# Tile places modulo 256 bytes, fifteen products of ones at the start, and the first weights ahead of the second part of x, in a two-layer encoder kernel

## The chip, the cores and the metric

The kernel runs on one core of a Trainium2 chip, in one launch. A core has TensorE (PE, matrix products; its weight loads are listed apart as PEld), VectorE (DVE), ScalarE (ACT), GpSimd (POOL) and SyncE (SP, which here issues all DMAs). The engines run side by side and wait for each other through semaphores. The metric is the device time of one execution in microseconds (us); lower is better.

## The reference, cut to what matters

Two layers on x of 512 tokens by 1024 features, all fp32. A layer has three attention branches, gates that mix them, and a squared-ReLU FFN:

```python
for l in range(2):
    h = rms_norm(x, norm_mix[l])
    u = h @ w_in[l]                               # one product, split into all that follows
    qa, ka, va, fa, qd, kvd, kr, qc, kc, vc, gl = split(u)
    ya = forgetting_attention(rms(qa), rms(ka), va, cumsum(log_sigmoid(fa + b)))
    yb = latent_attention(rms(qd) @ w_q_up, rms(kvd) @ w_kv_up, rope(kr))
    yc = chunk_attention(rms(qc), rms(kc), vc, rel_bias)
    merged = sum(sigmoid(gl_n + b_gate_n) * (y_n @ w_branch[n]))   # n = A, B, C
    x = x + merged @ w_out[l]
    h = rms_norm(x, norm_ffn[l])
    x = x + square(relu(h @ w_ff1[l])) @ w_ff2[l]
```

## The kernel before, in words

Each fp32 operand is split into a rounded high part and the rest (hi and lo, xgh and xgl, ah and al, mh and ml, yh and yl), both of type fp32r. A product of two split operands is three PE products of 128x128 weights with 512 moving columns: hi by hi, hi by lo, lo by hi. About 7000 of them make up the kernel.

All weight matrices lie in one DRAM array in the order of their use. `take` (line 127) brings the next 512 KB piece into a tile raw (line 137), ACT writes its rounded copy to whi (line 140) and DVE the rest to wlo (line 141). PE's program order is the order of the code; the other engines' order comes from a scheduler that goes by priorities. Tiles come from pools in SBUF (128 partitions; a tile takes the same bytes in each): the constants, w (raw, whi, wlo), xg (xgh, xgl: x times the norm's gain), t2 (temporaries), sm (small ones), and behind them pools that come and go with the stages: y and mg, mix, m (mh, ml), act (ah, al). A pool starts where the one before it ends, so the size of an earlier one sets where a later one lies. Two pools on the right side (xi, x) are placed from the other end.

The stages of a layer: projections for branch A (PE names ps_t, ps_k), the row norms (token sums ps_sum, line 292; then ps_r, line 320, which spreads them over the partitions with the constant onesr as weights and the tiles dg moving); attention A, C and B, each with gate tiles (ps_f), score products (ps_s), transposes (ps_p, ps_q), value products (ps_y) and branch projections (ps_b, line 802) between; the merge, which is the branch projection of B and the output projection (ps_o); and the FFN. In the FFN, 16 tiles of the first product (ps, moving xgh and xgl) alternate with 8 tiles of the second (ps, moving ah and al), twice a layer.

In most products the weights are the streamed tile (whi, wlo) and the activations move; in ps_t it is the other way round, xgh and xgl are the weights and whi, wlo move.

The program's start is in `run` (line 1000): SP issues the gains (vec), then the eight parts of x (xi, 256 KB each), with three prefetched weight pieces between (line 1018); the first piece comes in two halves. ACT and DVE split each part of x (`norm_split`, lines 272 and 273) and each weight piece. The first 72 products need three pieces and six parts of x, with the first piece used one part of x at a time.

Of the kernel before, what the change touches and what calls it, by code (L numbers as in the profile page):

```python
# [9 lines left out]
F32 = mybir.dt.float32  # L10
# [8 lines left out]
P = 128  # L19
T = 512  # L20
# [29 lines left out]
V_MIX, V_FFN, V_BG = 0, 8, 16  # L50
# [10 lines left out]
TUNE = dict(  # L61

    mla='ddddddddddddubuubu0qqqbbqqqqqbbuuuubqbbb1kbbktkkkbbbkkkbtbbgg',

    over=[1.0, 1.0, 1.0],

    na=10,

    tv=[13, 24],

    st=[0, 2, 4],

# [30 lines left out]
class Stream:  # L103


    def __init__(self, k, ap, layer):
        self.k, self.ap, self.layer, self.at, self.keys, self.pre = k, ap, layer, 0, [], []
# [39 lines left out]
class Fill:  # L147
# [10 lines left out]
    def run(self, ns):  # L158
        self.owed += ns
        while self.q and self.owed > 0:  # L160
            try:
                self.owed -= next(self.q[0])
            except StopIteration:
                self.q.pop(0)
        if not self.q:
            self.owed = 0.0
# [10 lines left out]
class Kern:  # L177
    def __init__(self, tc, ctx, a):
        self.tc, self.nc, self.a = tc, tc.nc, a
        self.ahead = TUNE["ahead"]  # L180
        self.fine = False
        self.ctx = ctx
        self.pc = self.pool(ctx, "const", 1)
        self.pw = self.pool(ctx, "w", 3)
        self.px = self.pool(ctx, "xg", 8)
        self.t2 = self.pool(ctx, "t2", 6)
        self.sm = self.pool(ctx, "sm", 2)
        self.dr = self.pool(ctx, "dr", 1, space=DRAM)
        self.mm = self.pool(ctx, "mm", 3, space=PSUM)
        self.pS = self.pool(ctx, "ps", 2, space=PSUM)  # L190
        self.pt = self.pool(ctx, "pt", 2, space=PSUM)
        self.py = self.pool(ctx, "py", 1, space=PSUM)

        self.sm.tile([P, 56], F32, tag="pad", name="pad", bufs=1)
        self.streams = [Stream(self, a["w"], l) for l in range(DEPTH)]
        self.vec = self.pc.tile([P, DEPTH, NV], F32, name="vec")

# [15 lines left out]
    def consts(self):  # L213
        nc, pc = self.nc, self.pc
        c = self.tmp()
        nc.sync.dma_start(out=c, in_=self.a["cst"])
        self.ident = pc.tile([P, P], F32, name="ident")
        self.li = pc.tile([P, 32], F32, name="li")
        nc.vector.memset(self.li, 0.0)
        nc.vector.tensor_copy(out=self.ident, in_=c[:, 0:128])  # L220
        self.maska = pc.tile([P, P], F32, name="maska")
        nc.vector.tensor_copy(out=self.maska, in_=c[:, 128:256])
        self.onesr = pc.tile([P, P], F32R, name="onesr")
        nc.vector.tensor_copy(out=self.onesr, in_=self.ones)
        self.hb = pc.tile([P, DEPTH, 24], F32, name="hb")
        nc.vector.tensor_scalar(out=self.hb, in0=self.vec[:, :, V_BG : V_BG + 24], scalar1=0.5, scalar2=None, op0=ALU.mult)
# [773 lines left out]
    def run(self):  # L1000
        nc = self.nc
        self.xd = self.dr.tile([P, KT, T], F32, name="xd")
        self.norm_begin()
        with ExitStack() as ctx:
            p0 = self.pool(ctx, "x0", 1, side="right")
            xs = [p0.tile([P, T], F32, name=f"xi{kt}") for kt in range(KT)]
            ahead, self.ahead = self.ahead, 0
            with self.tc.high_priority(100000):
                nc.sync.dma_start(out=self.vec, in_=self.a["vec"])
                self.ones = self.pc.tile([P, P], F32, name="ones")  # L1010
                nc.gpsimd.memset(self.ones, 1.0)
                warm = self.small(2, "warm", 1)
                nc.scalar.activation(out=warm, in_=self.ones[:, 0:2], func=AF.Copy)
                for kt in range(KT):
                    nc.sync.dma_start(out=xs[kt], in_=self.a["x"][:, kt])
                    self.norm_split(0, V_MIX, kt, xs[kt])
                    if kt in TUNE["st"]:
                        self.streams[0].prefetch(*self.first[TUNE["st"].index(kt)], pieces=1 if kt else 2)
            for kt in range(KT):
                self.norm_square(kt, xs[kt], nc.vector if kt % 2 else nc.gpsimd)  # L1020
            self.ahead = ahead
            self.consts()
        for l in range(DEPTH):
            yctx = ExitStack()
            self.ypool = self.pool(yctx, "y", 1)
            y = self.mixer(l)
            with ExitStack() as xctx:
                px = self.pool(xctx, "x", 1, side="right")
                x = [px.tile([P, T], F32, name=f"x{kt}") for kt in range(KT)]
                self.merge(l, y, x)  # L1030
                yctx.close()
                self.ffn(l, x)
# [98 lines left out]
```

## Time and profile before

| | us |
|---|---|
| three runs | 1844.39, 1841.53, 1840.97 |
| their median | 1841.53 |
| the profiled execution, its own time | 1842.65 |
| its span, from the first to the last instruction | 1840.9 |

| engine | busy us | share of the span |
|---|---|---|
| PE | 1808.0 | 98% |
| PEld | 1489.7 | 81% |
| DVE | 1056.5 | 57% |
| ACT | 784.6 | 43% |
| POOL | 216.7 | 12% |

The trace is of one execution. Products on PE are pipelined: the next one starts before the one before has ended, and the ends are modelled, so a row's duration (0.39 us for 512 columns) is not the time that the product costs; the distance between the starts of successive ones is. The mean granted clock of TensorE over the span is 0.996 of full speed.

### The profile page before, as it was taken

The page shows a single profiled execution, that of the slowest core. Times are in us where ns is not written, and L with a number is a line of the kernel's source. Part 1 is how long each engine was busy: PE and PEld are TensorE (multiplying, and loading weights), DVE is VectorE, ACT ScalarE, POOL GpSimd, SP SyncE. Part 2 cuts the span into 40 slices and gives each one's busy share as a digit, 9 for nine tenths or more (in the row PEclk, how much of TensorE's full clock was granted, in tenths as well). Part 3 has the DMA queues.
Part 4 walks back from the last instruction along what each step waited for, and adds up shares of the span by engine and source line. Part 5 has one row for each costly group of instructions (what it writes and reads, how often), then busy time and mean ns, then how long its engine had stood idle before and what let it go on. Part 6 is the DMA issues. An engine that isn't in the chain of part 4 may idle for free.

```text
span 1840.9 us, 23250 instructions
## 1 busy us (share of the span) xinstructions
PE 1808.0 (98%) x8496; PEld 1489.7 (81%) x8496; DVE 1056.5 (57%) x1994; ACT 784.6 (43%) x1369; POOL 216.7 (12%) x257
## 2 busy tenths in 40 slices
PE   8999999989999999999999999999899999999999
PEld 6888888868888888888888788888688888888887
DVE  7565477497765632553355654765977655325531
ACT  6565456446643222222245644664366432212311
POOL 1321200150011000000123202001500110000000
PEclk9999999999999999999999999999999999999999
DMA  5564365322353333333345633653234433333331
GB/s 179 157 167 122 104 182 143 121 94 87 114 167 92 94 101 92 93 102 109 109 125 144 172 109 108 185 146 118 86 92 141 135 92 103 93 92 97 97 115 58
DMA packets 84226, 217.85 MB, mean 118 GB/s; under 512 B 13696, under 2 KB 16768, under 8 KB 84112
## 3 DMA queue, kind: packets, MB, share of 16 engines
q1 hardware_dynamic: 84112, 216.37, 40.3%
q8 instruction: 67, 1.10, 0.2%
q14 instruction: 47, 0.39, 0.1%
HBM read 178.44 MB, written 12.71 MB: 104 GB/s over the span
## 4 chain that ended last, share of the span: by engine, by line
PE 87%; DVE 6%; ACT 3%; DMA 2%; issue 1%; SPq 1%; POOL 0%; DVEq 0%; ACTq 0%; POOLq 0%
PE ps L332 38%; PE ps_f L332 14%; PE ps_t L367 14%; PE ps_o L332 5%; PE ps_b L802 5%; PE ps_s L682 3%; PE ps_y L725 3%; PE ps_p L712 2%; PE ps_q L584 1%; DVE wlo L141 1%; SPq L599 1%; ACT whi L140 1%; DMA kl<-nat 1%; DMA cb<-cum 0%; PE ps_k L349 0%
## 5 line engine op out<-in xcount | busy, mean ns | idle before, releaser
L140 ACT ACTIVATE whi<-raw 128x1024 fp32r<-128x1024 f32 (+1 forms) x337 | 307.3, 919 | 771.8 <-issue 316.0
L141 DVE TENSOR_TENSOR wlo<-raw,whi 128x1024 fp32r<-128x1024 f32 (+1 forms) x337 | 358.9, 1069 | 253.2 <-ACT whi L140 237.6
L332 PE MATMUL ps<-ah,wlo 128*128 128x512 f32 x512 | 201.7, 394 | 0.0
L332 PE MATMUL ps<-ah,whi 128*128 128x512 f32 x512 | 201.7, 394 | 0.0
L332 PE MATMUL ps<-al,whi 128*128 128x512 f32 x512 | 201.7, 394 | 0.0
L332 PE MATMUL ps<-xgh,whi 128*128 128x512 f32 x512 | 199.4, 390 | 0.0
L332 PE MATMUL ps<-xgl,whi 128*128 128x512 f32 x512 | 199.2, 389 | 0.0
L332 PE MATMUL ps<-xgh,wlo 128*128 128x512 f32 x512 | 199.2, 389 | 0.0
L332 PE MATMUL ps_f<-xgh,whi 128*128 128x512 f32 x464 | 195.9, 422 | 0.0
L332 PE MATMUL ps_f<-xgh,wlo 128*128 128x512 f32 x464 | 182.5, 393 | 0.0
L332 PE MATMUL ps_f<-xgl,whi 128*128 128x512 f32 x464 | 182.1, 393 | 0.0
L367 PE MATMUL ps_t<-whi,xgh 128*128 128x512 f32 x384 | 151.4, 394 | 6.7 <-ACT whi L140 6.7
L367 PE MATMUL ps_t<-whi,xgl 128*128 128x512 f32 x384 | 150.2, 391 | 0.0
L367 PE MATMUL ps_t<-wlo,xgh 128*128 128x512 f32 x384 | 150.2, 391 | 0.0
L332 PEld LDWEIGHTS ps<-al,whi 128*128 128x128 f32 x512 | 95.7, 187 | 23.7
L332 PEld LDWEIGHTS ps<-ah,wlo 128*128 128x128 f32 x512 | 95.7, 187 | 23.7
L332 PEld LDWEIGHTS ps<-ah,whi 128*128 128x128 f32 x512 | 95.7, 187 | 23.7
L332 PEld LDWEIGHTS ps<-xgh,wlo 128*128 128x128 f32 x512 | 96.1, 188 | 20.1
L332 PEld LDWEIGHTS ps<-xgl,whi 128*128 128x128 f32 x512 | 96.1, 188 | 20.0
L332 PEld LDWEIGHTS ps<-xgh,whi 128*128 128x128 f32 x512 | 96.1, 188 | 19.9
L715 DVE TENSOR_TENSOR ptl<-ps_p,pth 128x512 fp32r<-128x512 f32 x144 | 85.9, 599 | 43.7 <-ACT pth L714 42.6
L956 DVE SCALAR_TENSOR_TENSOR t<-ps,rb 128x512 f32<-128x512 f32 x64 | 43.9, 691 | 114.2 <-PE ps L332 111.6
(196 smaller groups left out, 3202.8 us busy)
## 6 DMA issues: line engine op xcount, KB each, us to landing
raw<-w SPq DMA_DIRECT2D x277, 512.0 KB
qq<-nat SPq DMA_DIRECT2D x64, 128.0 KB
kk<-nat SPq DMA_DIRECT2D x64, 128.0 KB
kl<-nat SPq DMA_DIRECT2D x64, 128.0 KB
gd<-t SPq DMA_DIRECT2D x32, 256.0 KB
t<-rows SPq DMA_DIRECT2D x48, 128.0 KB
cb<-cum SPq DMA_DIRECT2D x16, 256.0 KB
cb<-gd SPq DMA_DIRECT2D x16, 256.0 KB
```

What stands on the lines that cost most here:

```text
L140: nc.scalar.activation(out=hi[:, c : c + v], in_=raw[:, c : c + v], func=AF.Copy)
L141: nc.vector.tensor_tensor(out=lo[:, c : c + v], in0=raw[:, c : c + v], in1=hi[:, c : c + v].bitcast(F32), op=ALU.subtract)
L332: nc.tensor.matmul(out=ps, lhsT=a[:, k], rhs=b[k], start=first and k == 0 and j == 0, stop=last and k == n - 1 and j == 2)
L367: nc.tensor.matmul(out=pss[t][:, 0:width], lhsT=a[k][:, t * P : t * P + P], rhs=b[:, i], start=c == 0 and i == 0 and j == 0, stop=last and ...
L584: nc.tensor.transpose(ps[0:rows, t * P : (t + 1) * P], src(t), self.ident)
L599: nc.sync.dma_start(out=s[rows, u].bitcast(F32), in_=x[own].bitcast(F32))
L682: nc.tensor.matmul(out=ps[:, 0:n], lhsT=a[:, i * P : (i + 1) * P], rhs=b[:, 0:n], start=j == 0, stop=j == len(terms) - 1)
L712: nc.tensor.transpose(ps[:, o + (i - kb) * P : o + (i - kb + 1) * P], pr[:, offs[i] + kb * P : offs[i] + (kb + 1) * P], self.ident)
L715: nc.vector.tensor_tensor(out=pl[:, 0:w], in0=ps[:, 0:w], in1=ph[:, 0:w].bitcast(F32), op=ALU.subtract)
L725: nc.tensor.matmul(out=yps[:, kb * P : T], lhsT=qkv[2][kb // 2][:, kb % 2, h, :], rhs=head[h][gi][x][:, o : o + T - kb * P], start=gi == 0 ...
L802: nc.tensor.matmul(out=pss[u], lhsT=chunk[a][:, u, k], rhs=y[b][k], start=k == 0 and j == 0, stop=k == 3 and j == 2)
L956: nc.vector.scalar_tensor_tensor(out=t, in0=ps, scalar=0.0, in1=self.rb, op0=ALU.max, op1=ALU.mult)
```

## The change

Three things. The tile li (128 bytes a partition, which takes the reciprocals of the softmax sums) moves from the constants to the small pool, and that pool's unused pad grows from 56 to 104 numbers (from 224 to 416 bytes). Fifteen products of the tile of ones with itself, 128 by 128 in fp32, stand first on PE; their result is not used. And at the start the pieces of weights are issued and converted right after the part of x they stood behind, before that part's split: the weights lead by one part of x.

```diff
     tv=[13, 24],
+    warm=15,
...
-        self.sm.tile([P, 56], F32, tag="pad", name="pad", bufs=1)
+        self.sm.tile([P, 104], F32, tag="pad", name="pad", bufs=1)
...
-        self.li = pc.tile([P, 32], F32, name="li")
+        self.li = self.sm.tile([P, 32], F32, tag="li", name="li", bufs=1)
...
                 nc.scalar.activation(out=warm, in_=self.ones[:, 0:2], func=AF.Copy)
+
+                ps = self.pt.tile([P, T], F32, tag="pt", name="ps_warm")
+                for _ in range(TUNE["warm"]):
+                    nc.tensor.matmul(out=ps[:, 0:P], lhsT=self.ones, rhs=self.ones, start=True, stop=True)
                 for kt in range(KT):
                     nc.sync.dma_start(out=xs[kt], in_=self.a["x"][:, kt])
-                    self.norm_split(0, V_MIX, kt, xs[kt])
                     if kt in TUNE["st"]:
                         self.streams[0].prefetch(*self.first[TUNE["st"].index(kt)], pieces=1 if kt else 2)
+                    self.norm_split(0, V_MIX, kt, xs[kt])
```

Where the tiles lie, as the two programs place them (byte address in a partition of the pool's first tile, and the address modulo 256, which all tiles of such a pool share):

| pool and tiles | before | mod 256 | after | mod 256 |
|---|---|---|---|---|
| constants: ones, ident | 16928 | 32 | 16928 | 32 |
| constants: onesr | 18592 | 160 | 18464 | 32 |
| w: raw, whi, wlo | 19296 | 96 | 19168 | 224 |
| xg: xgh, xgl | 56160 | 96 | 56032 | 224 |
| t2: t, dg | 88928 | 96 | 88800 | 224 |
| small: acc | 101440 | 64 | 101504 | 128 |
| y, mg; act: ah | 109856 | 32 | 110048 | 224 |
| mix: tok, pr, v, st, kk, qq; m: mh, ml; act: al | 142624 | 32 | 142816 | 224 |
| right side: xi, x | 212960 | 224 | 212960 | 224 |

On SP's queue the rows at the program's start, before (xi is a part of x, raw a piece or half a piece of weights):

```order
L1009 DMA vec<-vec 128x104
L1015 DMA xi_93<-x 128x512
L1015 DMA xi_94<-x 128x512
L137 DMA raw<-w 128x512 x2
L1015 DMA xi_95<-x 128x512
L1015 DMA xi_96<-x 128x512
L137 DMA raw<-w 128x1024
```

and after the change (the lines' numbers are those of the changed code):

```order
L1011 DMA vec<-vec 128x104
L1021 DMA xi_93<-x 128x512
L139 DMA raw<-w 128x512 x2
L1021 DMA xi_94<-x 128x512
L1021 DMA xi_95<-x 128x512
L139 DMA raw<-w 128x1024
L1021 DMA xi_96<-x 128x512
```

Each piece of weights has moved ahead of one part of x. ACT's rows at the same place, before (whi is the weights' rounded part, xgh that of x, acc and t are squares for the norm):

```order
L272 ACTIVATE xgh<-xi_93,vec 128x512
L280 ACTIVATE acc<-xi_93 128x512
L272 ACTIVATE xgh<-xi_94,vec 128x512
L140 ACTIVATE whi<-raw 128x512
L283 ACTIVATE t_168<-xi_94 128x512
L140 ACTIVATE whi<-raw 128x512
```

and after:

```order
L274 ACTIVATE xgh<-xi_93,vec 128x512
L282 ACTIVATE acc<-xi_93 128x512
L142 ACTIVATE whi<-raw 128x512 x2
L274 ACTIVATE xgh<-xi_94,vec 128x512
L285 ACTIVATE t_184<-xi_94 128x512
```

Both halves of the first weights now stand before the second part of x; on DVE the two wlo have moved in the same way. On PE the fifteen products are the only rows that are new, and the rest stands in the old order:

```order
L1122 UNCONDITIONAL_BRANCH
L1019 MATMUL ps_warm<-ones 128x128 x15
L369 MATMUL ps_t<-whi,xgh 128x512
L369 MATMUL ps_t<-whi,xgl 128x512
L369 MATMUL ps_t<-wlo,xgh 128x512
```

Nothing but the row of ps_warm differs on PE. From the token sums on, the orders of all five engines are those of before.

## Rows read from the trace of the kernel before

**Rows 1.** The page: engines' busy time, and the chain's shares by line.

```profile
PE 1808.0 (98%) x8496; PEld 1489.7 (81%) x8496; DVE 1056.5 (57%) x1994; ACT 784.6 (43%) x1369; POOL 216.7 (12%) x257
...
PE ps L332 38%; PE ps_f L332 14%; PE ps_t L367 14%; PE ps_o L332 5%; PE ps_b L802 5%; PE ps_s L682 3%; PE ps_y L725 3%; PE ps_p L712 2%; PE ps_q L584 1%; DVE wlo L141 1%; SPq L599 1%; ACT whi L140 1%; DMA kl<-nat 1%; DMA cb<-cum 0%; PE ps_k L349 0%
```

**Rows 2.** Waits of PE: whom for, us in total, times, longest.

```profile
PE ps_sum L292 <- DVE pr L461: 7.8, 2, 3.9
PE ps_t L367 <- ACT whi L140: 6.7, 1, 6.7
```

**Rows 3.** Groups of PE by form: shapes, count, busy us, mean ns, idle before.

```profile
L332 PE MATMUL ps<-ah,whi 128*128 128x512 f32 x512 | 201.7, 394 | 0.0
...
L332 PE MATMUL ps<-xgh,whi 128*128 128x512 f32 x512 | 199.4, 390 | 0.0
...
L802 PE MATMUL ps_b<-yh,whi 128*128 128x512 f32 x192 | 79.1, 412 | 0.0
...
L332 PE MATMUL ps_o<-mh,whi 128*128 128x512 f32 x128 | 50.5, 395 | 0.0
```

**Rows 4.** Timeline of PE, FFN second product: start us, duration, instruction.

```profile
689.64 0.39 PE L332 MATMUL ps<-al,whi 128*128 128x512 f32 x1
...
703.17 0.39 PE L332 MATMUL ps<-ah,wlo 128*128 128x512 f32 x1
```

**Rows 5.** Timeline of PE, FFN first product.

```profile
609.81 0.39 PE L332 MATMUL ps<-xgl,whi 128*128 128x512 f32 x1
...
623.64 0.39 PE L332 MATMUL ps<-xgh,wlo 128*128 128x512 f32 x1
```

**Rows 6.** Timeline of PE, merge: 62 products from the first to the last.

```profile
1429.65 0.39 PE L802 MATMUL ps_b<-yl,whi 128*128 128x512 f32 x1
...
1443.88 0.40 PE L332 MATMUL ps_o<-mh,wlo 128*128 128x512 f32 x1
```

**Rows 7.** Timeline of PE around the spreading of the row norms.

```profile
31.52 0.39 PE L367 MATMUL ps_t<-whi,xgh 128*128 128x512 f32 x1
...
32.20 0.63 PE L320 MATMUL ps_r<-dg,onesr 128*128 128x512 f32 x2
32.66 0.39 PE L367 MATMUL ps_t<-whi,xgh 128*128 128x512 f32 x1
...
34.05 0.39 PE L367 MATMUL ps_t<-whi,xgh 128*128 128x512 f32 x1
```

**Rows 8.** Timeline of PE in attention A, with one row in between left out.

```profile
100.26 0.60 PE L712 MATMUL ps_p<-ident,pr 128*128 128x128 f32 x4
...
100.87 0.33 PE L682 MATMUL ps_s<-kl,qq 128*128 128x384 f32 x1
101.04 0.40 PE L332 MATMUL ps_f<-xgh,whi 128*128 128x512 f32 x1
```

**Rows 9.** Timeline of PE at the start: the first product and the tenth.

```profile
6.73 0.80 PE L367 MATMUL ps_t<-whi,xgh 128*128 128x512 f32 x1 [6.73 <-ACT whi L140]
...
10.60 0.39 PE L367 MATMUL ps_t<-whi,xgh 128*128 128x512 f32 x1
```

**Rows 10.** Windows: stretch, length, busy and count by engine, PEclk, DMA share, GB/s.

```profile
387.83:392.60 4.77, 4.77 (x12) 3.78 (x13) 4.77 (x9) 0.00 (x0) 3.11 (x3) 0.50 0.50 137
```

**Rows 11.** Timeline of POOL, ACT and DVE at the start.

```profile
0.74 0.20 POOL L1011 MEMSET ones<- 128x128 f32 x1 [0.29 <-POOLq L1112]
...
5.46 0.71 ACT L272 ACTIVATE xgh<-xi,vec 128x512 fp32r<-128x512 f32 x1
...
6.07 0.61 ACT L140 ACTIVATE whi<-raw 128x512 fp32r<-128x512 f32 x1
...
7.78 0.63 ACT L140 ACTIVATE whi<-raw 128x512 fp32r<-128x512 f32 x1 [0.57 <-DMA raw<-w]
...
12.18 1.21 DVE L141 TENSOR_TENSOR wlo<-raw,whi 128x1024 fp32r<-128x1024 f32 x1
```

**Rows 12.** The tile ps_sum: records on PE, shortest, median, longest ns.

```profile
L292 PE MATMUL ps_sum<-ones,acc x32: 167/251/251, 24.9 to 1492.2; 128*128 128x2 f32 x32
```

## The prediction

> **What bounds the kernel now.** I read the page first. TensorE (PE) is busy 98% of the span, and the two FFN products (line 332, name ps) alone carry 38% of the chain that ended last [rows 1]. So only two things can change the time much: how soon PE starts, and how far apart its products start. The list of waits says that PE waits little: 6.7 us for the first weights, 7.8 us twice before the sums of the low-rank paths, and less elsewhere [rows 2]. The change touches the first of these.
>
> Then I read how far apart the starts of successive 128x512 products are, from the timeline; the duration of one is modelled and is longer than the distance. In the FFN's second product (moving operand ah or al) the first and the last of 59 products in a row start at 689.64 and 703.17: 13.53/58 = 0.2333 us each [rows 4]. In its first product (moving xgh or xgl) it is 62 products, 13.83/61 = 0.2267 us [rows 5]. In the merge (yh, yl, then mh, ml) it is 14.23/61 = 0.2333 again [rows 6]. Shape, type, instruction and weight buffers are the same in all three, and the queue waits for nothing. What differs is the pool of the moving tile: weights and xgh lie at 96 modulo 256, ah, al, yh, mh at 32 (the table of places in the section on the change). Like places give 0.2267, unlike ones 0.2333.
>
> Two more places bear on it. The products ps_r take weights from the constants at 160 and a moving tile at 96, both low in the memory. Before them three products take 0.68 us (0.2267 each); the two take 0.46; and the six behind them, whose operands are alike again, take 1.39, or 0.2317 each, before the pace comes back [rows 7]. So unlike places are slow without act or y tiles too, and a disturbance takes about six products to settle; ps_r stands at four places. In attention the gates' products come in threes between transposes and score products [rows 8], so they never settle.
>
> At the start PE begins at 6.73, when the first half of the weights is converted, and nine products take until 10.60, 0.43 each [rows 9]. That is the spacing of the stretch where the granted clock is 0.50, the 1.2 GHz level (12 products in 4.77 us, some cut by its edges) [rows 10]. The first products therefore run at half clock.
>
> **The change part by part.**
>
> *The places.* The constants lose the 128 bytes of li, and the small pool grows by 320. All pools that PE reads for large products then lie at 224: differences of 64 become zero. I price this by the pace of like places, 0.2267, in the stages where products follow each other without interruption:
> - FFN second product: 3 x 512 products [rows 3], each 0.2333 - 0.2267 = 0.0066 us: 10.1 us.
> - output projection: 3 x 128 [rows 3, 6]: 2.5 us.
> - the branch in the merge, a third of 3 x 192 [rows 3, 6]: 192 x 0.0066 = 1.3 us.
> Together 13.9 us, all on PE, which waits for nobody there. Nothing is late next: the FFN's first product already runs at 0.2267 with the same rate of weight transfers and conversions.
> - The two other branches' 384 products stand partly among other work: between 0 and 2.5 us; I take 1.5, since the merge's pace is the nearest row.
> - Gates and low-rank projections: 58 tiles of 24 products at like places before and after; they lose up to 1392 x 0.005 = 7 us against the settled pace. But transposes and short products stay between them. Between 0 and 7; I take 0.8, near the end of rows 7 and 8: they don't settle.
> The durations of ACT, DVE and POOL and the transfers I leave as they are; none of them bounds a stage where PE has the time.
>
> *The start.* Each product of ones is fp32: 16 such products of the program appear as 32 in the trace [rows 12], so 15 make 30. A 128-column one costs what a transpose costs, (101.04 - 100.26 - 0.17 - 0.17)/4 = 0.11 us at full clock [rows 8], 0.22 at half. They need only the tile of ones, ready at 0.94 [rows 11]. At half clock throughout they end at 0.94 + 6.6 = 7.5. If PE's clock rises as long after its first product as before (6.73 to 10.60, 3.87 us [rows 9]), 17 are done by 4.8 and the other 13 take 1.4: they end at 6.2.
> The weights now come before the second part of x on SP, ACT and DVE. On ACT the first whi stood behind the second xgh (5.46 to 6.07) [rows 11]; without it, it starts 0.61 earlier, and PE at 6.12 or just behind the ones. Nine products at 0.2267 instead of 3.87 us give back 1.83. Against that, x's second part now lands where the second half of the weights did, whose conversion began at 7.78 [rows 11]; its xgl is ready near 9.1, about when PE asks for it (6.12 + 13 x 0.227). PE asks for the second weights at 11.6 instead of about 14. Their low half was made from 12.18 to 13.39 [rows 11]; it moves one xgl (1.2 us) ahead, to about 12.2, and the next xgl comes at 13.0 to 13.4, against 12.05 and 12.8 asked. I count 1.1 us of waits: 0.61 + 1.83 - 1.1 = 1.3 us gained. Bounds: 2.4 (no waits) and -0.8 (ones end at 7.5 and the clock is no better then). From the token sums on, every queue has the old order.
>
> *The sum.* 13.9 + 1.5 + 0.8 + 1.3 = 17.5 us. The profiled execution took 1842.65 us (span 1840.9), so 1825.1. It lies 1.1 above the median of the runs shown, so I forecast 1824 for the median.
>
> **The rivals.**
>
> *Places don't matter.* The 0.0066 us may belong to the act and y pools for another reason, their height in the memory for one. Then only the start is left: 1841.5 - 1.3 = 1840.2. For it: all slow moving tiles but ps_r's lie high. Against it: ps_r, low and slow [rows 7]. The Trainium skill ("TensorE: Matmul & The Clock Gate", the step-by-step list of its Part 2) says that PE has two independent SBUF read ports, one for the streamed operand and one for the weights, so that loading the next weights doesn't take bandwidth from the running product. By that rule this rival holds; the trace's two paces for one instruction are not explained by it. Chance 11%.
>
> *Only part settles.* The stages with interruptions gain nothing and the FFN's second product half: 5 + 1.9 + 1.3 = 8 us: 1833. The rows that show like places at the good pace all have xgh or xgl as one operand. Chance 5%.
>
> *224 is a bad place (slower).* If what counts is where in 256 bytes the moving tile starts, not the difference, 96 may be good, and 224 as bad as 32. Then the products that are now at 0.2267 fall to 0.2333: FFN first 1536, ps_t with 512 columns 1152, the gates' 1392 in part: about 3000 x 0.0066 = 20 us, and nothing is gained elsewhere: 1841.5 + 20 - 1.3 = 1860. It turns slower than before once they lose more than 0.0005 us each. For it: no row shows anything at 224. Against: ps_r's moving tile lies at 96 and is slow, which speaks for the difference. Chance 6%.
>
> **How the numbers follow.** The forecast has 78%, its own range 1817 to 1831 (the open ends of attention, 0 to 9.5 us where I took 2.3, and of the start, and a few us between runs). The range 1815 to 1838 adds the partial rival; outside are the other two and the tails. About 0.2% (3.7 us) is what a measurement here can tell from no change. Faster by more: 78 + 5 + 1 = 84%. Within: 10%, nearly all of the rival without places. Slower: 6%.
>
> **What would show it.** Right: in the FFN's second product, the output projection and the merge successive products start 0.2267 apart; the FFN's first product stays there; ps_r and the six behind it keep their disturbance, 32 against 224. At the start 30 fp32 records from about 1.0 to about 6, the first ps_t near 6.1 and already 0.23 apart, with short waits for xgl and wlo before 14. Wrong: 0.2333 stays in these stages, or the FFN's first product slows, or the first ps_t comes after 7.

## The result, and the profile after

The changed kernel took 1827.36 us (median of five runs, 1825.38 to 1827.59) against 1841.53 (1840.89 to 1844.39): ratio 0.9916, 95% interval 0.9902 to 0.9929, so faster by 14.2 us. The forecast was 1824 in a range of 1815 to 1838. The profiled execution took 1825.38 us, 17.27 less than the one shown before (forecast 17.5). The two gains differ because the profiled execution of before lies 1.1 above its median and the profiled one of after 2.0 below its own.

The page of the changed kernel, the rows that answer to [rows 1]:

```profile
PE 1795.5 (98%) x8526; PEld 1495.0 (82%) x8526; DVE 1055.8 (58%) x1994; ACT 784.1 (43%) x1369; POOL 216.8 (12%) x257
...
PE ps L334 38%; PE ps_f L334 15%; PE ps_t L369 14%; PE ps_o L334 5%; PE ps_b L804 4%; PE ps_s L684 3%; PE ps_y L727 3%; PE ps_p L714 2%; DVE wlo L143 1%; PE ps_q L586 1%; SPq L601 1%; ACT whi L142 1%; DMA kl<-nat 1%; DMA kk<-nat 0%; PE ps_k L351 0%
```

PE has 30 instructions more and is busy 12.5 us less; DVE, ACT and POOL do what they did. The groups of PE by form (count, then busy us and mean ns), against [rows 3]:

```profile
L334 PE MATMUL ps<-xgh,whi 128*128 128x512 f32 x512 | 199.5, 390 | 0.0
...
L334 PE MATMUL ps<-ah,whi 128*128 128x512 f32 x512 | 199.2, 389 | 0.0
...
L804 PE MATMUL ps_b<-yh,whi 128*128 128x512 f32 x192 | 78.0, 406 | 0.0
...
L334 PE MATMUL ps_o<-mh,whi 128*128 128x512 f32 x128 | 49.8, 389 | 0.0
```

The two FFN products now cost the same. Their durations are modelled, so the spacing is what counts. PE's timeline in the FFN's second product, 112 products from the first row to the last (start, duration):

```profile
679.72 0.39 PE L334 MATMUL ps<-al,whi 128*128 128x512 f32 x1
...
704.88 0.39 PE L334 MATMUL ps<-al,whi 128*128 128x512 f32 x1
```

That is 25.16/111 = 0.2267 us, where [rows 4] had 0.2333. The first product, 68 of them:

```profile
609.23 0.39 PE L334 MATMUL ps<-xgh,wlo 128*128 128x512 f32 x1
...
624.42 0.39 PE L334 MATMUL ps<-xgh,whi 128*128 128x512 f32 x1
```

15.19/67 = 0.2267: it kept the pace of [rows 5] at its new place. The merge, 62 products as in [rows 6]:

```profile
1418.47 0.39 PE L804 MATMUL ps_b<-yl,whi 128*128 128x512 f32 x1
...
1432.30 0.39 PE L334 MATMUL ps_o<-mh,wlo 128*128 128x512 f32 x1
```

13.83/61 = 0.2267, from 0.2333. And the surroundings of ps_r, whose weights and moving tile are still unlike (32 and 224), against [rows 7]:

```profile
31.18 0.63 PE L322 MATMUL ps_r<-dg,onesr 128*128 128x512 f32 x2
31.64 0.39 PE L369 MATMUL ps_t<-whi,xgh 128*128 128x512 f32 x1
...
33.03 0.39 PE L369 MATMUL ps_t<-whi,xgh 128*128 128x512 f32 x1
```

The two take 0.46 and the six behind them 1.39, to the hundredth what they took before. (What that says of places is taken up behind the experiments.)

**Where the time came from.** For each tile name I summed, over all 512-column products whose distance to the next start is under 0.245 us, what that distance has above 0.2267. Before and after, in us: FFN 10.35 and 0.04; ps_o 2.55 and 0; ps_b 3.41 and 1.03; ps_f 4.89 and 4.60; ps_t 0.79 and 0.64; ps_y and ps_s 0.80 and 0.58. The differences add up to 15.9. The start gives 1.0 (the first token sums, ps_sum, begin at 23.89 against 24.91). The 0.4 that is left of the 17.27 are short stalls that come and go from run to run, below.

### The profile page after: what moved, and what is told of

It reads as the page before. It is cut to its first block, busy times and chain, and to the rows that moved or that the text cites. A ratio compares the mean times of both kernels' runs of the same rounds, so it can differ in the third digit from the quotient of the medians.

```text
span 1823.6 us, 23308 instructions
## 1 busy us (share of the span) xinstructions
PE 1795.5 (98%) x8526; PEld 1495.0 (82%) x8526; DVE 1055.8 (58%) x1994; ACT 784.1 (43%) x1369; POOL 216.8 (12%) x257
## 4 chain that ended last, share of the span: by engine, by line
PE 86%; DVE 6%; ACT 3%; DMA 2%; issue 1%; SPq 1%; POOL 0%; DVEq 0%; ACTq 0%
PE ps L334 38%; PE ps_f L334 15%; PE ps_t L369 14%; PE ps_o L334 5%; PE ps_b L804 4%; PE ps_s L684 3%; PE ps_y L727 3%; PE ps_p L714 2%; DVE wlo L143 1%; PE ps_q L586 1%; SPq L601 1%; ACT whi L142 1%; DMA kl<-nat 1%; DMA kk<-nat 0%; PE ps_k L351 0%
```

## The experiments

The theory: what a 512-column product costs goes by the distance between the places of its weights and of its moving tile in 256 bytes; the places give nearly all of the gain, the start about 1 us. The rivals: 224 is itself a good place, or a lower place in the memory is; the start gives more than I think; a smaller unit than 256 bytes decides.

A simple gauge for them all is one row of the chain of waits: the longest piece of it is the FFN of the first layer, 1467 products in a row, which hold all 768 of the second product (start, length). In the kernel before, and then after the change:

```profile
585.24 337.68 PE ps L332 x1467
```

```profile
581.71 332.55 PE ps L334 x1467
```

(337.68 - 332.55)/768 = 0.0067 us each, the same size as the 0.0066 read from the timelines.

**The places alone** (e1_places):

```diff
-        self.sm.tile([P, 56], F32, tag="pad", name="pad", bufs=1)
+        self.sm.tile([P, 104], F32, tag="pad", name="pad", bufs=1)
...
-        self.li = pc.tile([P, 32], F32, name="li")
+        self.li = self.sm.tile([P, 32], F32, tag="li", name="li", bufs=1)
```

> The places alone: li and the pad as in the change, the old start. By the difference theory (the pace of a product hangs on how far its weights and its moving tile lie apart modulo 256) the FFN's second product, the merge and the output projection go from 0.2333 to 0.2267 us a start, and the time falls by 14 to 16 us, to about 1826 to 1828; the first ps_sum stays near 25 us. If most of the gain came from the start, it stays above 1835.

Measured: 1827.62 us (1825.79 to 1830.36) against 1843.13, ratio 0.9916 (0.9905 to 0.9928). The FFN's piece of the chain:

```profile
584.63 332.54 PE ps L332 x1467
```

So the places alone give 15.5 us, all that the whole change gives as far as these runs can tell.

**The start alone** (e2_start): the ones and the new order of transfers, with every tile at its old place (pad of 56, li with the constants).

> The start alone: fifteen products of ones and the weights ahead, all tiles at the old places. By the difference theory the FFN's second product stays at 0.2333 us a start and the time falls by 1 to 2 us, to about 1840, hardly to be told from before; the first ps_sum comes near 24.0 us instead of 24.9. If the start mattered beyond its first 25 us, it would fall by more than 4 us.

Measured: 1842.70 us (12 runs) against 1843.13 (17 runs), ratio 0.9998 (0.9989 to 1.0006). The gain of the start lies between 2.0 us and a loss of 1.1; the runs don't show one. PE's timeline, and the FFN's piece of the chain:

```profile
7.14 0.48 PE L369 MATMUL ps_t<-whi,xgh 128*128 128x512 f32 x1
...
24.63 0.95 PE L294 MATMUL ps_sum<-ones,acc 128*128 128x2 f32 x8
```

```profile
585.82 337.68 PE ps L334 x1467
```

The old pace holds, and here the token sums begin 0.3 earlier than in before, not 1.0. In this execution the granted clock rose late, at 6.84, against 5.43 in the changed kernel's; more on that below.

**All pools at 96** (e3_all96): the pad of before with 72 numbers in place of 56; the tiles of act, y, mix and m move from 32 to 96, 64 bytes up, and so do the small tiles behind the pad (acc from 64 to 128); the weights and xgh stay.

> Everything alike, but at another place: the old start and li in the constants, the pad 16 numbers (64 bytes) longer than before, so that act, mix, y and m lie at 96 like the weights and xgh; acc lies at 128 as in the change. Difference theory: the same as the places alone, 0.2267 us a start in the FFN's second product, 1826 to 1828. If 224 itself is what helps: 0.2333 stays, 1841. If the height of the pools mattered: 0.2333 stays too, since act and y lie as high as before (64 bytes further).

Measured: 1828.47 us (4 runs), ratio 0.9922 (0.9909 to 0.9934). The chain's piece:

```profile
582.93 332.55 PE ps L332 x1467
```

Neither 224 as a place nor a lower place can be the cause: here the moving tiles went up, to 96, the weights stayed, and the pace is that of the changed kernel. Nor does a unit larger than 256 bytes show: from the first tile of w to the first of act it is 355 times 256 bytes in the changed kernel and 354 times here (the tiles of these pools, and the pieces of weights in a tile, are whole multiples of 512 bytes).

**Other distances.** Six times the kernel before with another pad, one profiled execution each. Three of them:

```diff
-        self.sm.tile([P, 56], F32, tag="pad", name="pad", bufs=1)
+        self.sm.tile([P, 104], F32, tag="pad", name="pad", bufs=1)   # e4; 88 in e5, 80 in e6
```

> Half the places: only the pad as in the change (104 numbers), li stays, so that the weights and xgh stay at 96 and act, mix, y and m lie at 224: 128 apart. If the pattern repeats every 128 bytes: 0.2267 us a start in the FFN's second product, as if alike. If it needs 256 bytes: another pace, 0.2333 or more, and about 1841 or above. If 224 for the moving tile is good whatever the weights' place: 0.2267.

> The kernel before with a pad of 88 numbers: weights and xgh at 96, act, mix, y and m at 160, the moving tile 64 above the weights (before: 64 below). Difference theory: any difference that is no multiple of 256 is slow, 0.2333 us a start in the FFN's second product, about 1841 to 1843. If the sign matters (the moving tile must not lie below): 0.2267.

> The kernel before with a pad of 80 numbers: weights and xgh at 96, act, mix, y and m at 128, 32 apart, the smallest step that the pools allow. If only exactly alike places help: 0.2333. If the cost grows with the distance: between 0.2267 and 0.2333, near 0.230.

and, with 64, 96 and 112 numbers:

> Before with 64 instead of 56 numbers in the padding tile: act, y and m tiles lie at 64 modulo 256, 32 below the weights' 96. Earlier runs gave a spacing in the FFN's second product of 0.2267 us at a distance of 0, 0.2333 at 64 below, at +32 and at +128, 0.2289 at +64. If every distance but 0 and +64 is slow: 0.2333, and the time of before within 2 us. If the good side is a band around 0 and +64 that reaches below: about 0.229, and some 10 us less than before.

> Before with 96 numbers in the padding tile: moving tiles of the second products at 192, 96 above the weights. If only 0 and +64 are better, 0.2333 in the FFN's second product and the time of before. If the cost goes by the distance from 0 or +64 in a graded way, between 0.2289 and 0.2333: 1832 to 1840.

> Before with 112 numbers in the padding tile: moving tiles of the second products at 0, 160 above (96 below) the weights. If only 0 and +64 are better: 0.2333 and the time of before. If what matters is that the moving tile starts a 256-byte row of the memory, 0.2267 and 1828.

The chain's piece for a moving tile 64 and then 160 bytes above the weights:

```profile
583.56 334.35 PE ps L332 x1467
```

```profile
586.12 338.43 PE ps L332 x1467
```

All together, with the place of the moving tile less that of the weights, modulo 256, and (piece - 332.55)/768 as the cost of one product:

| moving less weights | kernel | FFN piece, us | extra a product, ns | time, us |
|---|---|---|---|---|
| 0 | after, e3 | 332.55 | 0 | 1827.36, 1828.47 |
| 32 | e6 | 337.71 | 6.7 | 1841.11 |
| 64 | e5 | 334.35 | 2.3 | 1831.83 |
| 96 | e10 | 337.73 | 6.7 | 1844.43 |
| 128 | e4 | 337.66 | 6.7 | 1843.03 |
| 160 | e11 | 338.43 | 7.7 | 1844.27 |
| 192 | before | 337.68 | 6.7 | 1841.53 |
| 224 | e6b | 337.70 | 6.7 | 1842.48 |

The cost is not graded by distance: it is there at once at 32 on either side. It goes by 256 bytes and not by 128 (128 apart costs the full 6.7), and it has a sign, since 64 above costs a third of 64 below. I expected 0.2333 at 64 above and was wrong; e11's 160 is a shade worse than the rest, also unexpected. That a row of 256 bytes is met from its beginning is no help: e11's moving tile begins one.

**The two halves of the start.** e8_no_ones is the change without ps_warm; e7_ones_only keeps ps_warm and the places, but the parts of x and the weights have their old order:

```diff
                 for kt in range(KT):
                     nc.sync.dma_start(out=xs[kt], in_=self.a["x"][:, kt])
+                    self.norm_split(0, V_MIX, kt, xs[kt])
                     if kt in TUNE["st"]:
                         self.streams[0].prefetch(*self.first[TUNE["st"].index(kt)], pieces=1 if kt else 2)
-                    self.norm_split(0, V_MIX, kt, xs[kt])
```

> The change without the fifteen products of ones (places and weights ahead stay). PE starts near 6.3 instead of 6.47, but some nine or ten products run at 0.43 us a start, as before. First ps_sum near 25, against 23.9 with the ones and 24.9 before, if the ones bring the start's gain; near 24 if the earlier weights bring it.

> The change with the old order of transfers (each part of x is normed before the weights that follow it), so the ones and the places alone. If the ones bring the start's gain and the order nothing: first product of ps_t near 7.1 at full clock, token sums near 23.9, as in the change. If the earlier weights are needed too: token sums near 24.5, 0.6 later than in the change, as PE begins 0.6 later and the same weights end last. If the weights' earlier place costs more than it gives, token sums before 23.9.

Timelines of PE, without the ones, then with the ones alone:

```profile
6.64 0.80 PE L369 MATMUL ps_t<-whi,xgh 128*128 128x512 f32 x1 [6.64 <-ACT whi L142]
...
11.50 0.60 PE L369 MATMUL ps_t<-wlo,xgh 128*128 128x512 f32 x1
11.92 0.40 PE L369 MATMUL ps_t<-whi,xgh 128*128 128x512 f32 x1
...
25.56 0.84 PE L294 MATMUL ps_sum<-ones,acc 128*128 128x2 f32 x7
```

```profile
6.76 0.50 PE L369 MATMUL ps_t<-whi,xgh 128*128 128x512 f32 x1 [0.74 <-ACT whi L142]
...
23.64 0.95 PE L294 MATMUL ps_sum<-ones,acc 128*128 128x2 f32 x8
```

Without the ones PE's products stay 0.42 apart (the half-clock pace) until 11.92, and the token sums come at 25.56. With the ones and the old order they come at 23.64, 0.25 before those of the whole change. Each is one execution, and the granted clock rose at a different time in each: at 11.94 without the ones, 5.3 us after PE's first product, at 3.98 with the ones alone. So the 25.56 is in part a late rise. Two executions with the old start in which the clock rose as late, at 12.05 (e10) and 12.31 (e3), have their token sums at 25.72 and 25.84; beside these the earlier weights are worth 0.3 us at most. As far as single executions tell, what the start gains, the ones gain, and the weights' earlier place is not shown to buy anything. The times of the two, 1829.00 and 1829.78, can't tell a microsecond.

**Ones in the other long wait of PE** (e9_ones_in_wait), an attempt at a better version. Before the sums of the second low-rank path PE waits for about 4 us, once in each layer [rows 2], and the clock is at half speed after each wait. Sixteen more products of ones stand there:

```diff
-    def token_sums(self, *parts):
+    def token_sums(self, *parts, warm=0):
...
+        for _ in range(warm):
+            nc.tensor.matmul(out=ps[:, P : 2 * P], lhsT=self.ones, rhs=self.ones, start=True, stop=True)
...
-        s = self.token_sums(state["sq", part])
+        s = self.token_sums(state["sq", part], warm=16 * part)
```

> The change, and sixteen more products of ones right ahead of the token sums of the second low-rank path, in each layer, in columns of the same bank that nobody reads: PE waits there 4.14 us and then runs 6.83 us at the granted clock 0.50, twice. If idleness makes the clock fall: the ones fill some 3.5 of the 4.1 us (32 records of 0.11), the clock stays at 1.00, and each 6.83 us of work takes half: 6.8 us less in all, about 1820. If the clock falls for another reason, or the ones push the token sums back: 1827 or more.

Measured: 1829.69 us (1823.78 to 1830.62), ratio 0.9924 (0.9910 to 0.9938): no gain over the change is shown, and the forecast of 1820 failed. PE's waits in the changed kernel, then in e9 (us in total, times, longest):

```profile
PE ps_sum L294 <- DVE pr L463: 8.3, 2, 4.1
```

```profile
PE ps_sum L296 <- DVE pr L465: 1.2, 2, 0.6
```

Windows of both (length; busy and count of PE, PEld, DVE, ACT, POOL; granted clock; DMA share; GB/s). First the changed kernel, just behind that wait and over 32 us from its token sums:

```profile
384.50:391.20 6.70, 6.70 (x20) 5.64 (x21) 6.70 (x11) 0.00 (x0) 4.97 (x4) 0.50 0.36 108
...
384.40:416.40 32.00, 28.87 (x117) 22.91 (x118) 29.40 (x52) 12.83 (x20) 14.83 (x9) 0.89 0.26 82
```

then e9, the same 6.7 us, 32 us from its token sums (at 387.19), and 3.4 us within these:

```profile
384.50:391.20 6.70, 5.62 (x36) 4.37 (x36) 6.70 (x10) 1.27 (x2) 5.50 (x7) 1.00 0.16 30
...
387.20:419.20 32.00, 29.41 (x125) 22.23 (x126) 28.50 (x56) 13.96 (x25) 14.04 (x9) 0.95 0.35 105
...
412.30:415.70 3.40, 3.14 (x9) 1.95 (x8) 3.40 (x7) 1.20 (x2) 1.33 (x1) 0.50 0.00 0
```

The clock stays up where it fell before (1.00 for 0.50). PE's waits behind the sums don't grow: 3.1 us of these 32 in the changed kernel, 2.6 in e9. But 25 us later, behind several short waits, the clock falls after all, for 3.4 us (0.50), where it stayed at 1.00 in the changed kernel; why there is not shown. So it is low for half as long as before, and about half of the 3.4 us that I forecast for a layer is kept: from the start of the last branch product before the wait to the FFN it takes 182.7 us in place of 184.5, and the second layer gives 1.8 us too. The median doesn't show these 3.6 us. In the profiled execution 2.8 of them are lost to other stalls: from the first token sums to the second, where the programs are alike, it needs 329.2 us and the changed kernel 326.4.

**What hides a microsecond.** Starts compared product by product between e1's profiled execution (1830.36) and that of the change (1825.38): both do the same from the token sums on, yet single stalls in the attention stages differ. The largest, at the cumulated gates cb that a DMA brings, in e1 and then in the changed kernel (the bracket: idle before, and what ended it):

```profile
1008.38 0.46 POOL L685 TENSOR_TENSOR cb<-cb,maska 128x128 f32<-128x128 f32 x1 [5.07 <-DMA cb<-cum]
1008.88 0.69 DVE L691 CUSTOM_DVE_ANT_0 pr<-ps_s,cb 128x512 f32<-128x512 f32 x1 [2.73 <-POOL cb L685]
...
1011.92 0.63 PE L584 MATMUL ps_q<-ident,tok 128*128 128x128 f32 x4 [1.66 <-DVE ptl L715]
```

```profile
1007.88 0.88 POOL L687 TENSOR_TENSOR cb<-cb,maska 128x128 f32<-128x128 f32 x2 [2.66 <-DMA cb<-cum]
```

POOL waits 2.4 us longer for the same transfer, and PE loses 1.66 through DVE. From the first to the second token sums the profiled runs with like places need 325.6 (e3) to 329.2 us (e9) for the same work; a start that is 1 us earlier drowns in that.

## Why the prediction was right, and where not

- *The places, 13.9 us where products follow each other.* Right. FFN 10.3 (forecast 10.1), output projection 2.55 (2.5). The interrupted and uninterrupted branch products together gave 2.4, where I had 1.3 and 1.5. With the FFN at 10.3 the rival that only part settles is out.
- *The gates don't settle.* Right: ps_f still loses 4.60 of 4.89 us against the settled pace, though both operands lie alike. I gave gates and low-rank products 0.8; they gave 0.3.
- *Only the difference counts.* Right, as the FFN's first product showed at once, which keeps 0.2267 at a new place, and e3 at another place than the change's. The rival of 224 as a bad place is out by the same row. The rival that places don't matter is out as well (e1 against e2). The Trainium skill ("TensorE: Matmul & The Clock Gate", the step list of Part 2), which I had put beside it, has two independent read ports for weights and moving data; by that alone the table above would have one row, so it does not account for these paces. The step was too simple, though: at 64 above, unlike places cost only a third.
- *ps_r as a witness.* This reading of [rows 7] does not hold. No run lays the weights and the moving tile of ps_r alike, and the six products of 1.39 us stand behind other interruptions too, where all operands are alike. In the changed kernel, behind the waits for wlo and xgl, the last of which ends at 14.11:

```profile
14.11 0.39 PE L369 MATMUL ps_t<-wlo,xgh 128*128 128x512 f32 x1
...
15.50 0.39 PE L369 MATMUL ps_t<-wlo,xgh 128*128 128x512 f32 x1
...
16.18 0.39 PE L369 MATMUL ps_t<-wlo,xgh 128*128 128x512 f32 x1
```

Six products take 1.39, the next three 0.68, as around ps_r. That a disturbance takes six products to settle was right; that unlike places were this one's cause is not shown. The two rivals against which I held ps_r fell by the experiments.
- *The start, 1.3 us.* The ones worked as described; the term for the earlier weights, 0.61 us, was too large. The start of the changed kernel, PE, then ACT and DVE:

```profile
1.00 5.72 PE L1019 MATMUL ps_warm<-ones 128*128 128x128 f32 x30 [1.00 <-POOL ones L1013]
6.47 0.47 PE L369 MATMUL ps_t<-whi,xgh 128*128 128x512 f32 x1
...
7.36 0.39 PE L369 MATMUL ps_t<-whi,xgh 128*128 128x512 f32 x1
7.59 0.40 PE L369 MATMUL ps_t<-whi,xgl 128*128 128x512 f32 x1
...
13.11 0.50 PE L369 MATMUL ps_t<-wlo,xgh 128*128 128x512 f32 x1 [0.32 <-DVE wlo L143]
13.45 0.40 PE L369 MATMUL ps_t<-whi,xgh 128*128 128x512 f32 x1
13.78 0.50 PE L369 MATMUL ps_t<-whi,xgl 128*128 128x512 f32 x1
```

```profile
4.48 0.72 ACT L274 ACTIVATE xgh<-xi,vec 128x512 fp32r<-128x512 f32 x1 [2.24 <-DMA xi<-x]
...
5.63 1.14 ACT L142 ACTIVATE whi<-raw 128x512 fp32r<-128x512 f32 x2
...
10.59 1.06 ACT L142 ACTIVATE whi<-raw 128x1024 fp32r<-128x1024 f32 x1
```

```profile
11.69 1.37 DVE L143 TENSOR_TENSOR wlo<-raw,whi 128x1024 fp32r<-128x1024 f32 x1 [0.87 <-ACT whi L142]
```

The first part of x on ACT before the change, and then ACT in e8 (the new order without the ones):

```profile
4.31 0.72 ACT L272 ACTIVATE xgh<-xi,vec 128x512 fp32r<-128x512 f32 x1 [2.07 <-DMA xi<-x]
```

```profile
4.83 0.72 ACT L274 ACTIVATE xgh<-xi,vec 128x512 fp32r<-128x512 f32 x1 [2.59 <-DMA xi<-x]
...
5.97 1.13 ACT L142 ACTIVATE whi<-raw 128x512 fp32r<-128x512 f32 x2
```

The 30 records are there, the products behind them are 0.23 apart from 7.36 on, and PE waits twice before 14, for wlo and near an xgl. But the first ps_t comes at 6.47, not 6.12: the clock rose 4.43 us after PE's first product (at 5.43 in the trace's record of the granted clock), not 3.87, so more ones ran at half pace and PE got to its weights later than they were ready. Nor were the weights ready 0.61 earlier: I left the transfers as they were, but ACT gets the first part of x at 4.48 in the changed kernel and at 4.83 in e8, against 4.31 before, so that whi begins 0.44 and 0.10 earlier than at 6.07 [rows 11]. Over the ten executions with the old order of transfers that first row of ACT lies between 4.31 and 4.52, over the four with the new one between 4.48 and 4.83. And the second weights came later too: their ACT row begins at 10.59, so that wlo was ready near 13.1 and not at 12.2, and PE waits for it. The gain at the token sums was 1.0. Over three executions with this start (after, e9, e2) they begin at 24.1 on average, over nine with the old one at 25.1 (24.5 to 25.8). The timed runs neither show nor exclude it (e2).
- *The median.* Forecast 1824, measured 1827.36. The sum, 17.5, fits the 17.27 between the two executions with a profile, and that is partly luck: runs of one kernel lie 2 to 5 us apart, and what the parts measured adds up to 15.9 + 1.0 = 16.9. I took a profiled run to lie 1.1 above its median, and this one lies 2.0 below.
- *A slip in reading.* The 7.8 us of [rows 2] is the sum of two waits of 3.9, one in each layer, and not 7.8 twice. Nothing was worked out from it.

Not settled: what in the memory makes a product 0.0067 us longer, why 64 above is cheaper, and why a disturbance needs six products to go. The runs show the pattern and no cause. Every run also moves whole pools: raw, whi and wlo share one, so no run separates PE's read of the weights from what ACT, DVE and the DMAs write beside it. Against these writes speaks that the unlike pace of before is even: in the FFN's second product successive products there start 0.233 or 0.234 apart, all 1532 times, while the writes come and go.

## What to carry to other kernels

Where one engine's instruction has two paces in one trace, look at what differs between its stages in the allocation, not only in the program: here the same product cost 3% more at six of the seven distances modulo 256 bytes at which its weights and its moving tile lay apart (1% at the seventh), and a padding tile of another size was worth 15 us of 1842. Test such a reading by moving tiles to several distances, since one good and one bad place fit too many rules. And filling one wait to keep the clock up need not pay what the slow stretch behind it cost: here the clock fell again 25 us later, and half of the gain was left.

## What the runs showed of the hardware that I had not expected

- The cost of unlike places has a sign and steps: 0 at like places, 2.3 ns at 64 above, 7.7 at 160, 6.7 at the five other multiples of 32. The pace is not even at all of them: 128 apart (e4) the starts alternate between 0.229 and 0.238 us.
- The granted clock's first rise is not at a fixed time after PE's first product: 2.8 us (e6b), 3.68 (before), 4.43 (after), 5.3 (e8), 5.8 (e2). With the old start, late rises go with late token sums: a rise at 12.31 with sums at 25.84 (e3), one at 9.60 with 24.54 (e6b).
- In the changed kernel the clock was at its lower level for 6.8 us after each 4.1 us wait of PE (384.50 to 391.20 above); in some other executions (e5, e6 and e6b in the first layer) the 6.8 us came in two pieces with full clock between. Where the ones filled the wait it stayed up, and fell later, behind shorter waits of PE, for 3.4 us.
